# A hybrid decoder step: cached keys, convolution norm and opening put in another order

## The chip, the cores and the metric

The kernel runs on one core of one Trainium2 chip, as one program of some 14,900 instructions. The metric is the device time of one execution in microseconds; three executions of the kernel before gave 653.95, 655.58 and 656.63 us, median 655.58.

The core's engines each run their own list of instructions in order: PE (TensorE, matrix products), DVE (VectorE), ACT (ScalarE), POOL (GpSimd) and SP (SyncE, which here issues every DMA). They wait for each other by semaphores.

## The reference, cut to what matters

Two layers of a decoder for 512 prompt tokens and 8 samples of 4 tokens, all in float32. The change is in layer 0:

```python
q, k, v, g_att, u_a, u_b, g_conv = split(rms(x, norm_0) @ w_in_0)   # x: 544 x 1024
o_att  = attention of 8 heads: prompt tokens over themselves (causal),
         sample tokens over two cached pages of 128 keys and values each,
         found through page_table, and over their own 4 tokens
y      = conv1d(u_a * sigmoid(u_b), 31 taps, per channel) + conv_b
o_conv = silu(layernorm(y, conv_ln_g_0, conv_ln_b_0))
x      = x + concat(o_att * silu(g_att), o_conv * silu(g_conv)) @ w_out_0
```

Layer 1 is a gated linear recurrence (HGRN2) with a norm and two projections of its own; nothing of it is touched.

## The kernel before, in words

Tokens lie along the free axis: 544 columns in two halves of 272 (`HALF`, `HC`), with channels on the 128 partitions. A projection goes by weight tiles of 128 output columns. `wtile` (L127) loads one (tag `wr`, 3 buffers) and splits it in a high and a low part, the high one on ACT (L133), the low one on DVE (L134). `unit` (L137) makes one half of one output tile by 24 products (L142, L143, L144: high by high, high by low, low by high for 8 k-tiles) into a PSUM bank of tag `g`, of which there are 3. Attention scores use tag `s` (2 banks), transposes `t` (2), attention outputs `o` (1).

**Opening** (L247 to L311). `squares` (L256) sums the squares of x in four parts whose engine the tuples SQ and SQB give: `sqg` is a two-operand product on GpSimd (L186), `sqa` a Square on ACT (L180), `sqv` a product on DVE (L183). The parts are added at L265 (GpSimd), L266 and L267 (DVE). `norms` (L249) sums over partitions on PE (L252), takes the root on ACT and the reciprocal on DVE (L254): into `kr` for the first half, into `r1b` for the second. `rawsplit` (L270) makes the low part of the second half's x on DVE (L273), `wsplits` the low parts of the first two weight tiles (L282). `scaled` (L233, its product is L235) multiplies a finished PSUM tile by the norm: `ct` and `rs` are the results, and the PSUM bank is free only when they are made. `norm_a` (L285) multiplies the first half by its norm (L288).

**Middle of layer 0.** Four head pairs go through `prepkq`, `prepvg` and `attend` (L478: scores L484, mask L486, softmax, transposes of the probabilities L102, values L508), among them the convolution's inputs, `uconv`, and its taps on DVE. After the last `attend` (pair 3) stand `gates(0)` and `gates(1)`, two of four chunks of the convolution's gate (48 unit products each), then the layer norm of the convolution half by half: sum of channels, L565 on PE, subtraction and squares, L575 on PE, root, reciprocal. Then `gates(2)`, `gates(3)`, and a loop over chunks that makes the product with the gate (L582 to L595).

Then come the samples. The keys loop (L597) runs over two groups of four samples: 8 tiles of cached keys (tag `kn`, 8 buffers, 256 KB each; the page number is read by a TENSOR_LOAD on SP, L605, and the load is issued at L606), 32 products with the queries into a PSUM bank of tag `s` (L612), the mask (L616), the samples' own keys (L619), softmax and transposed probabilities `PT`. The values loop (L636) does the same with cached values: loads L646 into the same 8 `kn` buffers, products L639 and L651, then L661 gathers the heads. The layer norm's two accumulators take `kn` buffers too (L558), and so do the opening's squares and the two buffers of the convolution's state, which are in use till they are written out at L519 (`out_convs`). Then `w_out_0` is applied by units, and layer 1 follows.

**What sets the order.** The program is written once, in the order above; a scheduler with a model of the machine then sets each engine's list at build time, bound by `tc.issue_after` where the code names an instruction to come after. SP's list is in order too: a DMA that waits for its buffer holds all those behind it.

Of the kernel before, what the change touches and what calls it, by code (L numbers as in the profile page):

```python
# [13 lines left out]
AF = mybir.ActivationFunctionType  # L14
# [52 lines left out]
def hybrid_step(ctx, tc, xt_in, cache_kt, cache_v, conv_in, hgrn_in, page_table, par_in, k_norm_0,  # L67
# [59 lines left out]
    def wtile(w, col, k0=0, k1=KT):  # L127
        nk = k1 - k0
        raw = mk(wp, "wr", [128, nk, 128], 3)
        SP.dma_start(raw, w[col // 128, :, k0:k1, :])  # L130
        wh = mk(wp, "wh", [128, nk, 128], 3, F32R)
        wl = mk(wp, "wl", [128, nk, 128], 3, F32R)
        A.activation(wh, raw, AF.Copy)  # L133
        V.tensor_tensor(wl, raw, wh, op=ALU.subtract)  # L134
        return wh, wl, k0, k1

    def unit(w, a, hf):  # L137
        ps = bank("g", HALF)
# [18 lines left out]
    def vec(name, k=0):  # L157
        return vecs[:, vidx[name] + k:vidx[name] + k + 1]
# [15 lines left out]
    def mtile(key, dt=F32R):  # L174
        m_[key] = mk(hp, "m", [128, T], 2 * KT, dt)
        return m_[key]

    with tc.tile_pool(name="l0", bufs=1) as lp:
# [13 lines left out]
            V.tensor_scalar(xg[k][:, hs], xT[k][:, hs], vec("n0", k), None, op0=ALU.mult)  # L192

        SQ = (sqg, sqa, sqa, sqv)
        SQB = (sqg, sqa, sqa, sqv)
        XG = (xga, xgv, xga, xgv, xga, xgv, xga, xgv, )
        NM = (V, V, V, V, V, V, V, V, )
        xg = [mtile(("xg", k), F32) for k in range(KT)]
# [57 lines left out]
        def squares(hf):  # L256
            sq = []
            for i in range(4):
                q = mk(lp, "kn", [128, T], 8).rearrange("p (a t) -> p a t", a=2)
                (SQ, SQB)[hf][i](q, xTall[:, 2 * i:2 * i + 2, HC[hf]])  # L260
                sq.append(q)
                if hf == 0:
                    for k in (2 * i, 2 * i + 1):
                        XG[k](k, HC[0])
            G.tensor_tensor(sq[0], sq[0], sq[1], op=ALU.add)  # L265
            V.tensor_tensor(sq[2], sq[2], sq[3], op=ALU.add)  # L266
            V.tensor_tensor(sq[0], sq[0], sq[2], op=ALU.add)  # L267
            return sq[0]
# [266 lines left out]
        p3 = prepvg(*p3)  # L535
        taps(2)
        taps(3)
        pins = attend(*p3)
        gc = []

        def gates(c):
            w = wtile(w_in_0, 3072 + c * 128)
            g2 = up[c]
            for hf in range(2):
                with tc.issue_after(pins[0].ins):
                    ps = unit(w, h, hf)
                ps = scaled(ps, 1, 0) if hf else ps
                tg = mk(lp, "tb", [128, HALF], 3)
                A.activation(tg, ps, AF.Tanh, scale=0.5)
                V.scalar_tensor_tensor(g2[:, HC[hf]], tg, 1.0, ps, op0=ALU.add, op1=ALU.mult)  # L550
            gc.append(g2)

        gates(0)
        gates(1)
        rss = []
        at_ = [mk(lp, "kn", [128, T], 8) for _ in range(2)]
        accs = [[t[:, HC[hf]] for hf in range(2)] for t in at_]
        for hf in range(2):  # L558
            hs = HC[hf]
            acc = accs[0][hf]  # L560
            V.tensor_tensor(acc, cy[0][:, hs], cy[1][:, hs], op=ALU.add)
            for c in range(2, 4):
                V.tensor_tensor(acc, acc, cy[c][:, hs], op=ALU.add)
            pm = bank("g", HALF)
            PE.matmul(pm, ones, acc, start=True, stop=True)  # L565
            acc = accs[1][hf]
            for c in range(4):
                V.scalar_tensor_tensor(cy[c][:, hs], pm, -1.0 / 512, cy[c][:, hs], op0=ALU.mult, op1=ALU.add)
                sq = mk(lp, "ct", [128, HALF], 2) if c else acc
                A.activation(sq, cy[c][:, hs], AF.Square)  # L570
                if c:
                    V.tensor_tensor(acc, acc, sq, op=ALU.add)
            pq = bank("g", HALF)
            with tc.issue_after(pins[2 + hf].ins):
                PE.matmul(pq, ones, acc, start=True, stop=True)  # L575
            rs = mk(lp, "rs", [128, HALF], 2)
            A.activation(rs, pq, AF.Sqrt, scale=1.0 / 512, bias=eps)
            V.reciprocal(rs, rs)
            rss.append(rs)
        gates(2)  # L580
        gates(3)
        for c in range(4):  # L582
            tgs = []
            for hf in range(2):
                hs = HC[hf]
                V.scalar_tensor_tensor(cy[c][:, hs], cy[c][:, hs], vec("lg", c), rss[hf], op0=ALU.mult, op1=ALU.mult)
                V.tensor_scalar(cy[c][:, hs], cy[c][:, hs], vec("lb", c), None, op0=ALU.add)
                tg = mk(lp, "ct", [128, HALF], 2)
                A.activation(tg, cy[c][:, hs], AF.Tanh, scale=0.5)
                V.scalar_tensor_tensor(tg, tg, 1.0, cy[c][:, hs], op0=ALU.add, op1=ALU.mult)  # L590
                V.scalar_tensor_tensor(tg, tg, 0.25, gc[c][:, hs], op0=ALU.mult, op1=ALU.mult)
                tgs.append(tg)
            mh, ml = mtile(("h", 4 + c)), mtile(("l", 4 + c))
            for hf in range(2):
                split(mh[:, HC[hf]], ml[:, HC[hf]], tgs[hf])  # L595

        PTs = []  # L597
        for g in range(2):
            s = bank("s", 288)
            for j in range(2):  # L600
                kns = []
# [30 lines left out]
            A.activation(PT[:, :256], pT[:, :256], AF.Copy)  # L632
            A.activation(PT[:32, 256:384], pT[:32, 256:384], AF.Copy)
            PTs.append(PT)
        oms = []
        for g in range(2):  # L636
            PT = PTs[g]
# [443 lines left out]
```

## Time and profile before

| | us |
|---|---|
| three executions | 653.95, 655.58, 656.63 (median 655.58) |
| the profiled execution, its own time | 655.62 |
| its span, first to last instruction | 652.9 (2.7 lie around it) |
| PE busy | 629.5 (96%) |
| DVE busy | 524.8 (80%) |
| ACT busy | 365.5 (56%) |
| POOL busy | 62.7 (10%) |
| DMA, mean over the span | 108 GB/s |

The span is the execution on the time axis of the trace. Busy time of PE counts a product at the clock at which it ran; the trace shows that clock as a share of full speed (PEclk), where 1.00 is 2.4 GHz and 0.50 is 1.2 GHz.

### The profile page before, as it was taken

The numbers are of one execution on the slowest core, as the hardware profiler recorded it, in microseconds if no ns is written. First come the engines' busy times: TensorE is split into PE (matmuls) and PEld (weight loads), VectorE is DVE, ScalarE is ACT, GpSimd is POOL, SyncE is SP. The second block draws the span as 40 slices with busy tenths as digits, with TensorE's granted clock in tenths as the row PEclk, the third lists the DMA queues.
The fourth block names the chain that finished last, engine by engine and source line by source line (L and its number), as shares of the span: only waits on it lengthen the run. The fifth ranks groups of instructions, "written<-read, shape, count | busy, mean of one in ns | idle before, by whom it ended". The sixth has DMA issues, their size and how long they took to land.

```text
span 652.9 us, 14858 instructions
## 1 busy us (share of the span) xinstructions
PE 629.5 (96%) x5806; PEld 581.9 (89%) x5806; DVE 524.8 (80%) x1252; ACT 365.5 (56%) x908; POOL 62.7 (10%) x91
## 2 busy tenths in 40 slices
PE   8799999999999986999989999999999999999997
PEld 6699998997996855879989999999999999999997
DVE  6999989889889857666978988878787878866656
ACT  7344486487378674445755664646464646447321
POOL 6100000000100000000011211111111110121000
PEclk9799999999999997999999999999999999999999
DMA  8434311221242047446442232323223232322114
GB/s 297 121 82 111 113 56 66 84 83 65 80 84 81 22 139 241 155 143 213 162 146 102 70 113 84 107 93 102 99 99 102 84 117 69 115 78 94 46 58 149
DMA packets 39015, 70.56 MB, mean 108 GB/s; under 512 B 11938, under 2 KB 20642, under 8 KB 38946
## 3 DMA queue, kind: packets, MB, share of 16 engines
q1 hardware_dynamic: 38946, 69.63, 33.6%
q8 instruction: 45, 0.74, 0.5%
q14 instruction: 24, 0.20, 0.1%
HBM read 59.88 MB, written 9.73 MB: 107 GB/s over the span
## 4 chain that ended last, share of the span: by engine, by line
PE 88%; DVE 4%; DMA 3%; ACT 3%; SPq 1%; issue 1%; DVEq 0%; ACTq 0%
PE g L142 23%; PE g L143 23%; PE g L144 22%; PE t L102 5%; PE s L484 2%; PE o L508 2%; DMA kn<-in_cache_kt_dram 2%; PE o L952 1%; PE t L939 1%; PE s L847 1%; DMA kn<-in_cache_v_dram 1%; PE s L612 1%; PE s L853 1%; DMA xTall<-in_xt_dram 1%; PE o L954 1%
## 5 line engine op out<-in xcount | busy, mean ns | idle before, releaser
L142 PE MATMUL g<-h,wh 128*128 128x272 f32 x944 | 278.9, 296 | 5.3 <-DVE ct L235 2.7
L143 PE MATMUL g<-h,wh 128*128 128x272 f32 x944 | 277.9, 295 | 1.9 <-DVE h L273 1.7
L144 PE MATMUL g<-h,wl 128*128 128x272 f32 x944 | 275.4, 292 | 0.0
L142 PEld LDWEIGHTS g<-h,wh 128*128 128x128 f32 x944 | 179.7, 190 | 9.7 <-ACT f L743 3.1
L143 PEld LDWEIGHTS g<-h,wh 128*128 128x128 f32 x944 | 179.6, 190 | 6.0 <-DVE h L273 3.1
L144 PEld LDWEIGHTS g<-h,wl 128*128 128x128 f32 x944 | 179.5, 190 | 1.7 <-issue 1.2
L133 ACT ACTIVATE wh<-wr 128x1024 fp32r<-128x1024 f32 (+4 forms) x90 | 88.1, 981 | 91.1 <-PE g L143 84.5
L134 DVE TENSOR_TENSOR wl<-wr,wh 128x1024 fp32r<-128x1024 f32 (+4 forms) x90 | 101.1, 1125 | 26.4 <-ACT wh L133 25.6
L379 DVE SCALAR_TENSOR_TENSOR m<-m,vecs,m 128x512 f32<-128x512 f32 x120 | 87.5, 741 | 0.7
L142 PE MATMUL g<-m,wh 128*128 128x272 f32 x256 | 74.0, 293 | 0.3 <-ACT wh L133 0.3
L144 PE MATMUL g<-m,wl 128*128 128x272 f32 x256 | 74.1, 291 | 0.0
L143 PE MATMUL g<-m,wh 128*128 128x272 f32 x240 | 69.6, 290 | 0.0
L142 PEld LDWEIGHTS g<-m,wh 128*128 128x128 f32 x256 | 47.9, 188 | 2.6 <-DVE m L106 0.8
L144 PEld LDWEIGHTS g<-m,wl 128*128 128x128 f32 x256 | 48.1, 189 | 1.0 <-issue 0.8
L143 PEld LDWEIGHTS g<-m,wh 128*128 128x128 f32 x240 | 45.2, 188 | 1.1 <-DVE ct L590 0.8
L959 ACT ACTIVATE S<-S,tot 128x128 f32<-128x128 f32 x64 | 20.5, 390 | 11.4 <-PE t L858 11.4
L484 PE MATMUL s<-kz,qT 128*128 128x128 f32 (+3 forms) x64 | 22.8, 447 | 1.4 <-ACT PP L496 1.3
L916 DVE TENSOR_TENSOR qq<-qq,tot 128x256 f32<-128x256 f32 x24 | 11.7, 486 | 14.8 <-PE s L888 12.0
L503 ACT ACTIVATE PT<-t 128x128 f32<-128x128 f32 (+3 forms) x32 | 13.9, 433 | 14.7 <-PE t L102 14.6
L961 POOL TENSOR_TENSOR ve<-vx,cst 128x1024 fp32r<-128x1024 f32 x8 | 16.1, 2019 | 49.8 <-DVE vx L736 30.0
L1020 DVE TENSOR_TENSOR xTall<-g,xTall 128x272 f32<-128x272 f32 x32 | 13.5, 437 | 8.8 <-PE g L144 8.3
L917 DVE TENSOR_TENSOR kk<-kk,tot 128x256 f32<-128x256 f32 (+1 forms) x48 | 20.0, 417 | 0.3
(300 smaller groups left out, 1018.6 us busy)
## 6 DMA issues: line engine op xcount, KB each, us to landing
wr<-in_w_in_dram SPq DMA_DIRECT2D x58, 512.0 KB, 3.6
wr<-in_w_out_dram SPq DMA_DIRECT2D x16, 512.0 KB, 3.7
kn<-in_cache_kt_dram SPq DMA_DIRECT2D x16, 256.0 KB, 3.6
kn<-in_cache_v_dram SPq DMA_DIRECT2D x16, 256.0 KB, 4.7
S<-in_hgrn_dram SPq DMA_DIRECT2D x8, 512.0 KB, 4.8
out_hgrns_dram<-S SPq DMA_DIRECT2D x8, 512.0 KB, 2.6
xTall<-in_xt_dram SPq DMA_DIRECT2D x8, 272.0 KB, 5.4
out_y_dram<-xTall SPq DMA_DIRECT2D x8, 272.0 KB, 2.1
```

The costliest lines, as they stand in the source:

```text
L102: PE.transpose(out, in_, ident[:np_, :np_])
L133: A.activation(wh, raw, AF.Copy)
L134: V.tensor_tensor(wl, raw, wh, op=ALU.subtract)
L142: PE.matmul(ps, wh[:, k - k0, :], ah, start=(k == k0), stop=False)
L143: PE.matmul(ps, wh[:, k - k0, :], al, start=False, stop=False)
L144: PE.matmul(ps, wl[:, k - k0, :], ah, start=False, stop=(k == k1 - 1))
L379: V.scalar_tensor_tensor(cy[c][:, :TP], up[c][:, j:j + TP], cw[:, c, j:j + 1], cy[c][:, :TP], op0=ALU.mult, op1=ALU.add)
L484: sc = PE.matmul(ss[hh][:, :L], qT[:, i * 128:(i + 1) * 128], kT[:, hh, 0:L], start=True, stop=False)
L503: A.activation(PT[:, :L], pT[:, :L], AF.Copy)
L917: V.tensor_tensor(k3[:, :, 0, :], k3[:, :, 0, :], t3[:, :, 1:2].to_broadcast([128, nblk, hsz]), op=ALU.mult)
L959: A.activation(S0[:, n], S0[:, n], AF.Copy, scale=tots[:, n:n + 1])
L961: G.tensor_tensor(ve, vx.unsqueeze(1).to_broadcast([128, NS, 128]), exm.unsqueeze(2).to_broadcast([128, NS, 128]), op=ALU.mult)
```

## The change: keys(0) first, the norm in two parts, no GpSimd additions

Opening: the first quarter of the second half's squares goes from GpSimd to ACT (SQB); the addition L265 goes from GpSimd to DVE, for both halves; three casts of constants (L313, L315, L317) go from GpSimd to ACT.

Keys: the body of the keys loop becomes `keys(g)`. `keys(0)` is called ahead of the last pair's `attend`, `keys(1)` where the loop stood.

Norm: the means and squares of both halves come first, then `gates(2)`, then root and reciprocal of both halves, then `gates(3)`. The accumulators take tag `kr` (2 buffers) in place of `kn`.

```diff
-        SQB = (sqg, sqa, sqa, sqv)
+        SQB = (sqa, sqa, sqa, sqv)
...
-            G.tensor_tensor(sq[0], sq[0], sq[1], op=ALU.add)
+            V.tensor_tensor(sq[0], sq[0], sq[1], op=ALU.add)
...
-        G.tensor_copy(identb, ident)
+        A.activation(identb, ident, AF.Copy)
...
-        G.tensor_copy(causb, cst[:, C_CAUS:C_CAUS + 128])
+        A.activation(causb, cst[:, C_CAUS:C_CAUS + 128], AF.Copy)
...
-        G.tensor_copy(smb, cst[:, C_SM:C_SM + 64])
+        A.activation(smb, cst[:, C_SM:C_SM + 64], AF.Copy)
...
+        def keys(g):
...
+        keys(0)
         pins = attend(*p3)
         gc = []
...
-        at_ = [mk(lp, "kn", [128, T], 8) for _ in range(2)]
-        accs = [[t[:, HC[hf]] for hf in range(2)] for t in at_]
+        accs = [mk(lp, "kr", [128, T], 2) for _ in range(2)]
...
                 if c:
                     V.tensor_tensor(acc, acc, sq, op=ALU.add)
+        gates(2)
+        for hf in range(2):
             pq = bank("g", HALF)
             with tc.issue_after(pins[2 + hf].ins):
-                PE.matmul(pq, ones, acc, start=True, stop=True)
+                PE.matmul(pq, ones, accs[1][:, HC[hf]], start=True, stop=True)
...
-        gates(2)
         gates(3)
...
-        for g in range(2):
+        keys(1)
```

In the changed file the keys' loads are L548, their products L554, mask and own keys L558 and L561, the norm's products L605 and L617, the values' loads L650.

How the scheduler's order changes is shown at three places. Numbers after an underscore tell tiles of one name apart.

First, DVE in the opening, where the norm of the first half (`kr_107`) is applied to the first two PSUM tiles (`g_156`, `g_170`). Before:

```order
L273 SCALAR_TENSOR_TENSOR h_93<-xTall,vecs,h_85 128x272
L267 TENSOR_TENSOR kn_195<-kn_195,kn_199 128x544
L273 SCALAR_TENSOR_TENSOR h_94<-xTall,vecs,h_86 128x272
L254 RECIPROCAL kr_107<-kr_107 128x272
L273 SCALAR_TENSOR_TENSOR h_95<-xTall,vecs,h_87 128x272
L134 TENSOR_TENSOR wl_357<-wr_354,wh_356 128x1024
L254 RECIPROCAL r1b<-r1b 128x272
L235 TENSOR_TENSOR ct_214<-g_156,kr_107 128x272
L235 TENSOR_TENSOR rs_216<-g_170,kr_107 128x272
```

With the change:

```order
L254 RECIPROCAL kr_107<-kr_107 128x272
L267 TENSOR_TENSOR kn_195<-kn_195,kn_199 128x544
L273 SCALAR_TENSOR_TENSOR h_93<-xTall,vecs,h_85 128x272
L273 SCALAR_TENSOR_TENSOR h_94<-xTall,vecs,h_86 128x272
L273 SCALAR_TENSOR_TENSOR h_95<-xTall,vecs,h_87 128x272
L134 TENSOR_TENSOR wl_357<-wr_354,wh_356 128x1024
L235 TENSOR_TENSOR ct_214<-g_156,kr_107 128x272
L235 TENSOR_TENSOR rs_216<-g_170,kr_107 128x272
L288 TENSOR_TENSOR tb_218<-m_99,kr_107 128x272
L288 TENSOR_TENSOR tb_222<-m_100,kr_107 128x272
L288 TENSOR_TENSOR tb_226<-m_101,kr_107 128x272
L254 RECIPROCAL r1b<-r1b 128x272
```

The reciprocal of the second half, `r1b`, stood ahead of the two L235 and stands now behind them and three L288. Each L265, not shown here, stands some rows further up on DVE, the second one behind the first two L273.

Second, PE in attention, where before the keys of both groups (`s_3091`, `s_3242`) follow the last values product (L508) of pair 3:

```order
L508 MATMUL o_2563<-PT_2684,vt_2421 64x128
L508 MATMUL o_2563<-PT_2698,vt_2421 64x128
L508 MATMUL o_2563<-PT_2684,vt_2421 64x128
L508 MATMUL o_2563<-PT_2698,vt_2421 64x128
L612 MATMUL s_3091<-kn_3125,qbd 32x128
L612 MATMUL s_3091<-kn_3114,qbd 32x128
L612 MATMUL s_3091<-kn_3103,qbd 32x128
L612 MATMUL s_3091<-kn_3092,qbd 32x128
```

With the change the end of keys(0), whose PSUM tile is `s_2563`, stands ahead of the first scores of pair 3 (`s_2715`):

```order
L554 MATMUL s_2563<-kn_2657,qbd 32x128
L554 MATMUL s_2563<-kn_2646,qbd 32x128
L102 MATMUL t_2296<-cst,PP_2292 128x128 x4
L554 MATMUL s_2563<-kn_2635,qbd 32x128
L554 MATMUL s_2563<-kn_2624,qbd 32x128
L558 LDWEIGHTS identb
L558 MATMUL s_2563<-smb,identb 128x32
L561 MATMUL s_2563<-ksT,qbd 32x32 x16
L484 MATMUL s_2715<-kz_486,qT_2092 128x128
L486 LDWEIGHTS identb
```

The 32 products of keys(0) run from 42 rows above these last ones, among the last transposes and L508 of pair 2. Those of keys(1) (`s_3242`) stand as 8 after both L605, 12 between the two L617 and 12 after the units of `gates(3)`, followed by the values.

Third, SP around the cached keys. Before, all 16 loads stand behind the fourth tile of `w_out_0`:

```order
L130 DMA wr_3614<-in_w_out_dram 128x1024
L130 DMA wr_3647<-in_w_out_dram 128x1024
L382 DMA out_convp_dram<-m_275 128x30
L464 DMA out_v_prompt_dram<-vt_2421 128x4x128
L465 DMA out_v_sample_dram<-vsn 32x128
L130 DMA wr_3682<-in_w_out_dram 128x1024
L130 DMA wr_3717<-in_w_out_dram 128x1024
L606 ISA
L606 DMA kn_3092<-in_cache_kt_dram 128x512
```

With the change:

```order
L519 DMA out_convs_dram<-kn_268 128x16x30
L548 ISA
L548 DMA kn_2657<-in_cache_kt_dram 128x512
L130 DMA wr_3032<-in_w_in_dram 128x1024
L130 DMA wr_3106<-in_w_in_dram 128x1024
L439 DMA out_k_prompt_dram<-kt_2069 128x4x128
L440 DMA out_k_sample_dram<-kt_2069 32x128
L130 DMA wr_3614<-in_w_out_dram 128x1024
L130 DMA wr_3647<-in_w_out_dram 128x1024
L548 ISA
L548 DMA kn_3243<-in_cache_kt_dram 128x512
```

Six loads of keys(0) are not in this piece: they stand in the opening, behind `wr_492`, and the seventh behind the first `out_convs`. The eighth (`kn_2657`) stands right behind the second `out_convs`, which writes out the buffer that it takes. The eight of keys(1) stand behind two tiles of `w_out_0`, no longer four.

## Rows read from the trace of the kernel before

**Rows 1.** The page, part 1: busy us, share of the span, instructions.

```profile
PE 629.5 (96%) x5806; PEld 581.9 (89%) x5806; DVE 524.8 (80%) x1252; ACT 365.5 (56%) x908; POOL 62.7 (10%) x91
```

**Rows 2.** Timeline of PE, opening: start us, us, engine, line, tiles [idle<-releaser].

```profile
25.98 0.59 PE L142 MATMUL g<-h,wh 128*128 128x272 f32 x1 [2.68 <-DVE ct L235]
```

**Rows 3.** Windows of four stretches: us, PE, PEld, DVE, ACT, POOL, PEclk, DMA, GB/s.

```profile
21.00:23.30 2.30, 1.43 (x8) 0.92 (x6) 2.30 (x3) 0.57 (x2) 0.11 (x1) 1.00 0.07 29
23.30:25.90 2.60, 0.01 (x1) 0.00 (x0) 2.60 (x4) 0.98 (x1) 0.00 (x0) 0.77 0.00 0
25.90:31.30 5.40, 5.32 (x23) 5.32 (x24) 5.02 (x13) 1.57 (x4) 0.00 (x0) 0.50 0.34 114
60.00:100.00 40.00, 40.00 (x319) 38.87 (x318) 36.99 (x73) 24.62 (x47) 0.22 (x1) 1.00 0.32 100
```

**Rows 4.** Timeline of DVE in the opening.

```profile
7.52 1.27 DVE L192 TENSOR_SCALAR m<-xTall,vecs 128x272 f32<-128x272 f32 x1 [0.89 <-DMA xTall<-in_xt_dram]
...
9.35 0.35 DVE L192 TENSOR_SCALAR m<-xTall,vecs 128x272 f32<-128x272 f32 x1
...
11.08 3.25 DVE L282 TENSOR_TENSOR wl<-wr,wh 128x1024 fp32r<-128x1024 f32 x2
14.25 2.47 DVE L273 SCALAR_TENSOR_TENSOR h<-xTall,vecs,h 128x272 fp32r<-128x272 f32 x3
...
17.32 0.49 DVE L273 SCALAR_TENSOR_TENSOR h<-xTall,vecs,h 128x272 fp32r<-128x272 f32 x1
17.73 0.71 DVE L266 TENSOR_TENSOR kn<-kn,kn 128x544 f32<-128x544 f32 x1
...
22.66 1.21 DVE L134 TENSOR_TENSOR wl<-wr,wh 128x1024 fp32r<-128x1024 f32 x1
23.80 1.84 DVE L254 RECIPROCAL r1b<-r1b 128x272 f32<-128x272 f32 x1
```

**Rows 5.** Timeline of POOL (GpSimd) in the opening.

```profile
7.07 1.34 POOL L265 TENSOR_TENSOR kn<-kn,kn 128x544 f32<-128x544 f32 x1 [1.47 <-ACT kn L180]
...
11.07 2.17 POOL L186 TENSOR_TENSOR kn<-xTall 128x544 f32<-128x544 f32 x1 [2.43 <-DMA xTall<-in_xt_dram]
13.32 2.21 POOL L265 TENSOR_TENSOR kn<-kn,kn 128x544 f32<-128x544 f32 x1
```

**Rows 6.** Timeline of PE, end of the third head pair.

```profile
212.82 0.49 PE L484 MATMUL s<-kz,qT 128*128 128x128 f32 x2 [0.62 <-ACT PP L496]
```

**Rows 7.** Timeline of PE around the keys and the convolution norm.

```profile
241.47 0.66 PE L102 MATMUL t<-cst,PP 128*128 128x128 f32 x4 [1.13 <-ACT PP L498]
242.26 0.73 PE L575 MATMUL g<-kn,ones 128*128 128x272 f32 x2
...
245.55 1.08 PE L612 MATMUL s<-kn,qbd 128*32 128x128 f32 x32 [1.08 <-DMA kn<-in_cache_kt_dram]
249.62 1.62 PE L612 MATMUL s<-kn,qbd 128*32 128x128 f32 x32 [2.99 <-DMA kn<-in_cache_kt_dram]
...
253.88 1.94 PE L612 MATMUL s<-kn,qbd 128*32 128x128 f32 x32 [1.91 <-DMA kn<-in_cache_kt_dram]
255.75 1.24 PE L575 MATMUL g<-kn,ones 128*128 128x272 f32 x2
```

**Rows 8.** Timeline of PE around the cached values.

```profile
270.38 0.46 PE L619 MATMUL s<-ksT,qbd 128*32 128x32 f32 x32
...
272.46 1.12 PE L639 MATMUL s<-vsn,PT 32*128 32x512 f32 x2
...
277.95 1.06 PE L651 MATMUL s<-kn,PT 128*32 128x512 f32 x8 [0.58 <-DMA kn<-in_cache_v_dram]
```

**Rows 9.** Timeline of SP, which issues the DMAs.

```profile
179.56 0.38 SPq L519 DMA_DIRECT2D out_convs_dram<-kn  x1
...
239.00 17.16 SPq L606 DMA_DIRECT2D kn<-in_cache_kt_dram  x16
...
270.34 2.00 SPq L646 DMA_DIRECT2D kn<-in_cache_v_dram  x4
```

More of the change, by code (lines that the diff above doesn't have):

```diff
@@ L537, in hybrid_step @@
         taps(3)
[L538 to L551, printed above, removed]
@@ L553, in hybrid_step @@
-        gates(0)
-        gates(1)
-        rss = []
-        at_ = [mk(lp, "kn", [128, T], 8) for _ in range(2)]
-        accs = [[t[:, HC[hf]] for hf in range(2)] for t in at_]
[L558 to L574, printed above, removed]
-                PE.matmul(pq, ones, acc, start=True, stop=True)
[L576 to L579, printed above, removed]
@@ L580, in hybrid_step @@
-        gates(2)
[L581 to L595, printed above, removed]
@@ L634, in hybrid_step, with gates @@
             PTs.append(PT)
+        keys(0)
+        pins = attend(*p3)
+        gc = []
+        def gates(c):
+            w = wtile(w_in_0, 3072 + c * 128)
+            g2 = up[c]
+            for hf in range(2):
+                with tc.issue_after(pins[0].ins):
+                    ps = unit(w, h, hf)
+                ps = scaled(ps, 1, 0) if hf else ps
+                tg = mk(lp, "tb", [128, HALF], 3)
+                A.activation(tg, ps, AF.Tanh, scale=0.5)
+                V.scalar_tensor_tensor(g2[:, HC[hf]], tg, 1.0, ps, op0=ALU.add, op1=ALU.mult)
+            gc.append(g2)
@@ new lines, in hybrid_step @@
+        gates(0)
+        gates(1)
+        rss = []
+        accs = [mk(lp, "kr", [128, T], 2) for _ in range(2)]
+        for hf in range(2):
+            hs = HC[hf]
+            acc = accs[0][:, hs]
+            V.tensor_tensor(acc, cy[0][:, hs], cy[1][:, hs], op=ALU.add)
+            for c in range(2, 4):
+                V.tensor_tensor(acc, acc, cy[c][:, hs], op=ALU.add)
+            pm = bank("g", HALF)
+            PE.matmul(pm, ones, acc, start=True, stop=True)
+            acc = accs[1][:, hs]
+            for c in range(4):
+                V.scalar_tensor_tensor(cy[c][:, hs], pm, -1.0 / 512, cy[c][:, hs], op0=ALU.mult, op1=ALU.add)
+                sq = mk(lp, "ct", [128, HALF], 2) if c else acc
+                A.activation(sq, cy[c][:, hs], AF.Square)
+                if c:
+                    V.tensor_tensor(acc, acc, sq, op=ALU.add)
@@ new lines, in hybrid_step @@
+        gates(2)
+        for hf in range(2):
+            pq = bank("g", HALF)
+            with tc.issue_after(pins[2 + hf].ins):
+                PE.matmul(pq, ones, accs[1][:, HC[hf]], start=True, stop=True)
+            rs = mk(lp, "rs", [128, HALF], 2)
+            A.activation(rs, pq, AF.Sqrt, scale=1.0 / 512, bias=eps)
+            V.reciprocal(rs, rs)
+            rss.append(rs)
+        gates(3)
+        for c in range(4):
+            tgs = []
+            for hf in range(2):
+                hs = HC[hf]
+                V.scalar_tensor_tensor(cy[c][:, hs], cy[c][:, hs], vec("lg", c), rss[hf], op0=ALU.mult, op1=ALU.mult)
+                V.tensor_scalar(cy[c][:, hs], cy[c][:, hs], vec("lb", c), None, op0=ALU.add)
+                tg = mk(lp, "ct", [128, HALF], 2)
+                A.activation(tg, cy[c][:, hs], AF.Tanh, scale=0.5)
+                V.scalar_tensor_tensor(tg, tg, 1.0, cy[c][:, hs], op0=ALU.add, op1=ALU.mult)
+                V.scalar_tensor_tensor(tg, tg, 0.25, gc[c][:, hs], op0=ALU.mult, op1=ALU.mult)
+                tgs.append(tg)
+            mh, ml = mtile(("h", 4 + c)), mtile(("l", 4 + c))
+            for hf in range(2):
+                split(mh[:, HC[hf]], ml[:, HC[hf]], tgs[hf])
```

## The prediction, made before the changed kernel ran

> **What bounds the kernel now.** I read the page's busy shares first: PE is busy 96% of the span, some 23 us short of all of it [rows 1]. A change that takes no product away can therefore win little more than PE's idle time and the time in which PE ran at half clock. So the next view is PE's own timeline, read for the idle time in front of each instruction and for what ended it. The two largest clusters lie where the change works. In the opening PE stops for 2.68 us until DVE has made `ct` at L235 [rows 2]. Around 241 to 256 it stops four times, 1.13, 1.08, 2.99 and 1.91 us, once for the softmax of the last pair and three times for cached keys that have not landed [rows 7]. The windows view tells the second part of the price: PEclk is 1.00 up to 23.3, 0.77 on the mean of the 2.68 us stop, and 0.50 for 5.40 us after it, the lower of the two levels [rows 3]. The same shows in the keys: 32 products that take 1.08 us at the first wait take 1.62 and 1.94 after the 2.99 us one [rows 7]. So each long stop is paid twice. Between 60 and 100 PE has no gap at all [rows 3], and nothing is to be had there.
>
> **The opening.** L235 reads a PSUM tile and frees its bank; the product at 25.98 needs that bank. DVE works without a pause ahead of it, so L235 comes as much earlier as DVE's list ahead of it gets shorter.
> - GpSimd's three two-operand pieces (7.07, 11.07 and 13.32) go [rows 5]. The DVE work that ran beside them is long: L192 1.27 us where one alone takes 0.35, two L282 3.25 where the same shape at L134 takes 1.21 each, three L273 2.47 where one alone takes 0.49 [rows 4, 5]. If they run at the lone price, 0.9, 0.8 and 1.0 us go: −2.7. The nearest other reading is that they were slow for a reason of their own, then this is 0.
> - The reciprocal `r1b`, 1.84 us, stood ahead of L235 and now stands behind it [rows 4]: −1.8. Nothing needs it before the next L235, which belongs to the product after.
> - DVE gets two additions L265. Their price is that of L266, the same shape: 0.71 [rows 4]. The second costs it in full. The first falls into the 0.89 us that DVE waits for x in front of 7.52 [rows 4]; GpSimd could start it at 7.07 [rows 5], so some 0.2 remains. Together +0.9.
> - ACT gets one square and three casts. It is busy 0.57 and 0.98 us of the 2.30 and 2.60 ahead of the stop [rows 3], so they cost nothing; without that cover they would delay a weight split by about a microsecond.
>
> That makes −3.6: the product starts at about 22.4. PE gets two new, shorter stops on the way, since the second half's norm now waits on DVE's L267: by my walk down DVE's list about 1.7 us and 0.6 us. The decision is whether they drop the clock. The 2.68 us stop did [rows 2, 3]; between 21.0 and 23.3 PE was busy only 1.43 of 2.30 us, and the clock stayed at 1.00 [rows 3]. I take the row that is nearer in total idleness, the second: no drop. Then the products between 25.9 and 31.3 run at the full rate: 24 of them in 5.40 us are 0.225 each, 319 in 40.00 are 0.125 [rows 3], so another −2.4. Against it stands DVE, 5.02 busy of those 5.40 us and 36.99 of 40 later [rows 3]: a PE that is 6 us ahead must be followed by DVE, whose reserve is some 3 us in 40. I take 1.3 us as given back (bounds 0 and 3). **Opening: −3.6 − 2.4 + 1.3 = −4.7**, between −1 and −6.4.
>
> **The keys and the norm.** Of the 16 key tiles, loaded from 239.0 in 17.16 us behind four tiles of `w_out_0` [rows 9], seven now land far ahead; the eighth is a rival below. The six loads in the opening add 1.5 MB to a stretch in which the DMA engines moved 29 and 0 GB/s [rows 3], and their page numbers are read by SP as before. The loads of keys(1) wait only for keys(0)'s buffers, which come free some 20 us before their products. So three DMA waits go, and the softmax wait at 241.47 is filled with the units of `gates(2)`, which now stand ahead of that transpose: 1.13 + 1.08 + 2.99 + 1.91 = −7.1 [rows 7]. With the 2.99 us stop its half clock goes: 0.54 + 0.86 on the keys, and 1.24 against 0.73 on the two L575: −1.9 [rows 7].
>
> keys(0) itself is only moved. It stands where PE waits 0.62 us for probabilities [rows 6], and fills that; but its softmax holds one of two score banks, which the second score of pair 3 needs, for about as long. I take 0, between −0.6 and +1.5. The norm in two parts moves root and reciprocal behind 48 unit products (6 us of cover) and makes DVE do nothing more.
>
> What is late next is the cached values. They need the buffers of keys(1), so they are issued when its last product is done. Before, issue began at 270.34 and the product that needed them came at 277.95 after a wait [rows 8, 9]: 7.6 us. In the new order PE has less to do in that time: the own keys 0.46, L639 1.12, the first L651 1.06 [rows 8] and 26 unit products of 0.125, 5.9 together, so 1.7 us of wait. The second group's later half is issued when that L651 is done; until its own L651 stand 19 unit products (2.4), L661 (about an L639, 1.1), three transposes (0.5, by the four of [rows 7]), L639 and half the L651 (1.1 each), 6.2 together: 1.4 us of wait. Before, this stretch had 0.58 [rows 8]. So +2.5, between 0 and +5 (other loads beside them). Of these the price 7.6 is the measured one. By the Trainium skill (DMA: Bandwidth & Descriptors, Specifications) SP's path takes about 0.6 us to the first byte, and HBM gives one core about 358 GB/s; four tiles, 1.05 MB, would by that be an estimated 3.5 us, and both waits would be nothing. The rows say twice that, and I follow them.
>
> **Middle: −7.1 − 1.9 + 2.5 = −6.5**, between −3 and −10.
>
> Layer 1 stands in the same order as before and only comes earlier. The sum is −11.2 against the profiled execution's 655.6, which stands at the median of the three runs (655.58): **644.4 us**.
>
> **The rivals.**
> - *Loads as fast as the memory allows.* If the values land in the time of their bytes, the 3.1 us of waits in the sum go: 641.3. Against it stand the 7.6 us of the rows [rows 8, 9].
> - *The opening gives nothing.* Its two new stops, 2.3 us in a stretch of some 5, drop the clock as the 2.68 us did, and DVE, which is nearly full there, eats the start that came earlier. Only the middle remains: 655.6 − 6.5 = 649.1. For it speaks PEclk 0.77 within one stop [rows 3]. By the Trainium skill (TensorE: Matmul & The Clock Gate, Part 1) "the default state is throttled, and activity releases the throttle", so a thin stretch would do it without one long stop; the 1.43 us in 2.30 at 1.00 [rows 3] do not show that.
> - *The middle gives nothing.* The waits for keys come back as waits for values, softmax banks or weight tiles behind the earlier loads in SP's queue: 655.6 − 4.7 = 650.9. For it: all 16 value tiles still go through the same eight buffers. Against it: weight tiles are loaded ahead, and 48 products of 0.125 per tile are 6 us each.
> - *Nothing to measure.* The scheduler has moved half of PE's list; if small waits spread over it eat what both parts win, the time stays within 3.3 us of 655.6. Against it: PE was gapless in such stretches before [rows 3].
> - *Slower.* The eighth tile `kn_2657` takes the buffer that the second `out_convs` writes out. That write was issued at 179.56 [rows 9]; write and load, at 7.6 us each, end at about 195. PE needs it at about 206, where pair 2 ends, and all behind it on PE waits with it. From 206 on each microsecond later is lost, and by 220 the 11.2 us are used up and 3.3 more lost: 659 and over. Nothing moves `out_convs` by 25 us in DVE's order, so this is unlikely.
>
> **How the numbers follow.** About 0.5% (3.3 us) is what a measurement of this kernel can tell from no change. Chances: the forecast 0.50, fast loads 0.08, opening lost 0.16, middle lost 0.10, nothing to measure 0.11, slower 0.05. So faster 0.84, same 0.11, slower 0.05. The range reaches from the fast loads with the better opening, 639.0, to the middle lost, 651.0; it leaves out the last two cases. The forecast's own range is 641 to 648.
>
> **What the new profile would show.** Right: no stop of 2.7 us for L235, the first unit products after it at about 22.4 with PEclk 1.00; DVE's L282 at 1.2 and L273 at 0.5; no wait of the keys' products for a DMA; 240 to 256 without a gap; one or two waits of 1 to 2 us in front of L651. Wrong: PEclk 0.50 somewhere before 30; a wait for the eighth tile near 206; more than 5 us of waits for values; DVE as the releaser of many small PE waits between 30 and 200.

## The result, and the profile after

The changed kernel takes 643.64 us (median of four executions, 641.23 to 647.24) against 654.81 of the kernel before in the same runs: ratio 0.9842, 95% interval 0.9818 to 0.9865. The two medians lie 11.2 us apart, and the ratio makes it 10.3 us (8.8 to 11.9); forecast were 11.2. The profiled execution took 643.47, its span is 641.6 against 652.9.

Where it came from is read from one fixed place. The two norm products that close layer 0, one per half, are L685 before and L689 now; the last record of the second starts at 339.2 before and at 328.1 now. So 11.1 of the 11.3 us that the span lost lie ahead of it, and layer 1 gave 0.2. The first scores of pair 0, which close the opening, start at 83.20 before and at 77.70 now: 5.5 us are from the opening and the other 5.6 from the middle.

The page's first part, beside [rows 1]: PE is busy for 3.5 us less, though its instructions are the same 5806, since fewer of them ran at half clock.

```profile
PE 626.0 (98%) x5806; PEld 580.0 (90%) x5806; DVE 522.2 (81%) x1254; ACT 367.5 (57%) x912; POOL 52.1 (8%) x85
```

**The opening.** PE's timeline of the changed kernel, beside [rows 2]:

```profile
19.55 1.16 PE L252 MATMUL t<-kn,ones 128*128 128x272 f32 x4 [1.97 <-DVE kn L267]
...
22.52 0.40 PE L142 MATMUL g<-h,wh 128*128 128x272 f32 x1 [0.80 <-DVE ct L235]
```

The product behind L235 starts at 22.52, 3.5 us earlier. The new stop in front of L252 is there too, 1.97 us, and another of 0.80. The windows, as in [rows 3] (us, PE, PEld, DVE, ACT, POOL, PEclk, DMA share, GB/s), show that they cost no clock, although PE was busy for only 0.58 of 2 us in the first and 1.20 of 2 in the third:

```profile
17.00:19.00 2.00, 0.58 (x5) 0.36 (x3) 2.00 (x2) 1.29 (x3) 0.59 (x1) 1.00 1.12 156
...
21.00:23.00 2.00, 1.20 (x9) 0.98 (x8) 2.00 (x4) 1.29 (x2) 0.00 (x0) 1.00 0.83 259
23.00:25.00 2.00, 2.00 (x19) 2.00 (x17) 2.00 (x4) 1.13 (x3) 0.00 (x0) 1.00 0.79 247
```

DVE's timeline, beside [rows 4], shows the prices without GpSimd beside it:

```profile
7.34 0.73 DVE L265 TENSOR_TENSOR kn<-kn,kn 128x544 f32<-128x544 f32 x1 [0.39 <-ACT kn L180]
7.99 0.36 DVE L192 TENSOR_SCALAR m<-xTall,vecs 128x272 f32<-128x272 f32 x1
...
10.56 2.35 DVE L282 TENSOR_TENSOR wl<-wr,wh 128x1024 fp32r<-128x1024 f32 x2
12.83 0.91 DVE L273 SCALAR_TENSOR_TENSOR h<-xTall,vecs,h 128x272 fp32r<-128x272 f32 x2
13.66 0.72 DVE L265 TENSOR_TENSOR kn<-kn,kn 128x544 f32<-128x544 f32 x1
...
22.03 0.43 DVE L235 TENSOR_TENSOR ct<-g,kr 128x272 f32<-128x272 f32 x1
```

L192 takes 0.36 us where it took 1.27, two L282 2.35 where they took 3.25, and each L265 about 0.72, as forecast from L266.

**The middle.** PE's timeline, beside [rows 6] and [rows 7] (in the changed file the keys' products are L554, the norm's L605 and L617, the values' L643 and L655):

```profile
204.49 1.50 PE L554 MATMUL s<-kn,qbd 128*32 128x128 f32 x44 [0.21 <-ACT PP L496]
```

```profile
233.23 1.08 PE L605 MATMUL g<-kr,ones 128*128 128x272 f32 x4
...
244.51 0.86 PE L554 MATMUL s<-kn,qbd 128*32 128x128 f32 x24
...
253.19 0.86 PE L554 MATMUL s<-kn,qbd 128*32 128x128 f32 x24
```

```profile
268.29 1.06 PE L655 MATMUL s<-kn,PT 128*32 128x512 f32 x8 [0.67 <-DMA kn<-in_cache_v_dram]
...
274.56 1.00 PE L142 MATMUL g<-m,wh 128*128 128x272 f32 x3 [1.31 <-ACT m L105]
```

No product of the keys waits for a DMA any more. The windows of the same stretch show no idle time from 240 to 260, and then what came in exchange: 1.4 us of idle time between 270 and 275, and the clock at 0.50 for some 6 us.

```profile
240.00:250.00 10.00, 10.00 (x98) 8.59 (x97) 5.67 (x9) 7.94 (x12) 0.00 (x0) 1.00 0.44 149
250.00:260.00 10.00, 10.00 (x120) 7.83 (x118) 9.53 (x20) 4.56 (x7) 0.00 (x0) 1.00 0.59 193
260.00:265.00 5.00, 4.67 (x36) 3.49 (x36) 4.75 (x14) 2.47 (x8) 0.00 (x0) 1.00 0.94 322
...
270.00:275.00 5.00, 3.58 (x25) 3.06 (x24) 4.51 (x17) 2.73 (x10) 0.00 (x0) 0.96 0.01 3
275.00:280.00 5.00, 4.86 (x20) 4.22 (x20) 4.27 (x7) 3.91 (x6) 0.00 (x0) 0.50 0.12 41
```

SP's timeline, beside [rows 9]: the eighth tile was issued at 181.10, when the write in front of it had landed, and the eight tiles of keys(1) at 205.58, 28 us ahead of their first product. The values behind them go from 245.17 on, the last twelve tiles at 254.06 and 261.13.

```profile
181.10 0.35 SPq L548 DMA_DIRECT2D kn<-in_cache_kt_dram  x1
...
205.58 5.16 SPq L548 DMA_DIRECT2D kn<-in_cache_kt_dram  x8
...
254.06 4.95 SPq L650 DMA_DIRECT2D kn<-in_cache_v_dram  x8
...
261.13 2.34 SPq L650 DMA_DIRECT2D kn<-in_cache_v_dram  x4
```

### The profile page after: what moved, and what is told of

Its sections match the earlier page's. It is cut to its first block, busy times and chain, and to the rows that moved or that the text cites. A ratio compares the mean times of both kernels' runs of the same rounds, so it can differ in the third digit from the quotient of the medians.

```text
span 641.6 us, 14859 instructions
## 1 busy us (share of the span) xinstructions
PE 626.0 (98%) x5806; PEld 580.0 (90%) x5806; DVE 522.2 (81%) x1254; ACT 367.5 (57%) x912; POOL 52.1 (8%) x85
## 4 chain that ended last, share of the span: by engine, by line
PE 87%; DVE 5%; ACT 3%; DMA 2%; issue 1%; SPq 1%; DVEq 0%; ACTq 0%
PE g L142 23%; PE g L143 22%; PE g L144 22%; PE t L102 5%; PE s L484 2%; PE o L508 2%; DMA wr<-in_w_in_dram 1%; PE o L956 1%; PE t L943 1%; PE s L851 1%; PE s L857 1%; PE o L958 1%; PE s L554 1%; DMA kn<-in_cache_v_dram 1%; PE t L862 1%
## 5 line engine op out<-in xcount | busy, mean ns | idle before, releaser
L142 PE MATMUL g<-m,wh 128*128 128x272 f32 x256 | 74.7, 299 | 1.4 <-ACT m L105 1.3
L143 PE MATMUL g<-m,wh 128*128 128x272 f32 x240 | 70.7, 296 | 0.1
L142 PEld LDWEIGHTS g<-m,wh 128*128 128x128 f32 x256 | 48.7, 193 | 4.4 <-issue 1.7
L143 PEld LDWEIGHTS g<-m,wh 128*128 128x128 f32 x240 | 46.4, 194 | 0.7 <-DVE m L106 0.3
```

## The experiments

Each kernel computes everything. "Close" is the place named above, the last record of the norm product that closes layer 0, in the profiled execution; what lies behind it took 312.0 to 315.2 us in these traces. Ratios are to the kernel before, run beside each on the same chip; its medians there were 654.07 to 656.18, so ratios and closes compare better than the medians of different rows.

| kernel | median us | ratio (95%) | close, us |
|---|---|---|---|
| before | 654.81 | 1 | 339.2 |
| the change | 643.64 | 0.9842 (0.9818 to 0.9865) | 328.1 |
| opening alone | 649.67 | 0.9917 (0.9891 to 0.9943) | 334.1 |
| middle alone | 650.43 | 0.9920 (0.9896 to 0.9945) | 332.6 |
| change, norm in its old order | 650.31 | 0.9909 (0.9880 to 0.9939) | 333.8 |
| change, keys(0) late | 643.26 | 0.9794 (0.9767 to 0.9822) | 327.4 |
| opening and kr accumulators alone | 649.61 | 0.9930 (0.9911 to 0.9949) | 332.6 |
| opening and split norm alone | 642.98 | 0.9827 (0.9806 to 0.9848) | 326.6 |
| change, accumulators in kn | 642.94 | 0.9817 (0.9797 to 0.9836) | 327.9 |
| opening alone, norm products in t | 647.24 | 0.9896 (0.9871 to 0.9921) | 331.7 |
| change, GpSimd's work back | 650.27 | 0.9928 (0.9905 to 0.9952) | 334.8 |
| change, L659 held back | 639.47 | 0.9778 (0.9761 to 0.9794) | 323.7 |
| the same, lb on ACT | 638.39 | 0.9767 (0.9744 to 0.9789) | 322.1 |
| the same, keys(0) late | 638.98 | 0.9756 (0.9736 to 0.9776) | 323.3 |

### The two halves apart

Opening alone: the first five edits of the change, on the kernel before.

> The opening's edits alone, the middle as before. Theory A, two separate gains: in the trace with the change the product behind L235 starts 3.5 us earlier and the 24 products behind it run at the full clock (2.4 us), and the third head pair's rows are then 5.5 to 6.7 us early, so DVE gives nothing back. By A this kernel takes 654.8 - 5.9 = 649 us, the product starts at 22.5 with a wait under 1 us, and PEclk is 1.00 till 35. Rival B, DVE gives back what PE gains, and the early rows come only from a reordered list: 651.5 to 653 us, with new waits of PE for DVE between 30 and 200.

Middle alone: the changed kernel with those five edits undone.

```diff
-        SQB = (sqa, sqa, sqa, sqv)
+        SQB = (sqg, sqa, sqa, sqv)
...
-            V.tensor_tensor(sq[0], sq[0], sq[1], op=ALU.add)
+            G.tensor_tensor(sq[0], sq[0], sq[1], op=ALU.add)
...
-        A.activation(identb, ident, AF.Copy)
+        G.tensor_copy(identb, ident)
```

> Keys and norm as in the change, the opening as before. Theory A: 654.8 - 5.3 = 649.5 us; the three waits for cached keys are gone, and the half clock after 274 of the changed kernel (a wait of 1.3 us for the last chunk of the convolution, then 6 us at 0.50) is there, some 6 us later. Rival B, the middle needs the opening (with the six key loads in a free stretch of SP and DVE's list early): under 3 us of gain, 652 us or more, with key tiles late. Rival C, the half clock at 274 is a by-product of the early opening and is not here: 646 to 647 us.

The closes are 5.1 and 6.6 us early, 11.7 together, and the change's is 11.1 early: the two halves add (A). Of the 6.6, 0.9 stand already at pair 0 (82.33 for 83.20), from the scheduler's other order; so 5.7 are the middle's own, as the change's 5.6. In the opening alone pair 0's first scores stand at 77.66, as in the change, so DVE gave nothing back there. The 0.4 us between 5.5 and 5.1 are less than the waits for keys grew with an earlier PE: 1.25, 3.46 and 2.65 us, 7.4 in all, where the kernel before had 1.08 + 2.99 + 1.91 [rows 7].

In the middle alone the stop for the convolution's last chunk is there, 1.32 us, as in the change; but the clock holds (that part of C is seen, its total is not):

```profile
280.85 0.65 PE L142 MATMUL g<-m,wh 128*128 128x272 f32 x3 [1.32 <-ACT m L105]
```

```profile
280.00:282.00 2.00, 1.15 (x8) 1.10 (x9) 1.53 (x5) 0.99 (x3) 0.00 (x0) 1.00 0.00 0
282.00:284.00 2.00, 1.05 (x6) 0.61 (x6) 2.00 (x4) 2.00 (x3) 0.00 (x0) 1.00 0.00 0
```

### Which edit of the middle it is

Norm in its old order, keys(0) early:

```diff
-        gates(2)
-        for hf in range(2):
             pq = bank("g", HALF)
...
             rss.append(rs)
+        gates(2)
         gates(3)
```

> The changed kernel with the convolution's norm in its old order: half by half with root and reciprocal, then the gate chunks 2 and 3; keys(0) stays early, and the accumulators stay in their new buffers. Theory A: the early keys carry the gain of the middle (6.0 us of waits for keys and 1.4 of half clock) and the split norm only fills one wait of 1.1 us: 643.6 + 1 to 2, 644.6 to 645.6 us. Rival: the norm in two parts is what keeps PE filled between 240 and 255; without it PE waits twice for root and reciprocal (two table loads of 1.3 us and 1.85 us each on the way): 647 us or more, with PEclk falling there.

Keys(0) late, norm split:

```diff
-        keys(0)
         pins = attend(*p3)
...
+        keys(0)
         keys(1)
```

> The changed kernel with keys(0) called right ahead of keys(1), where the loop stood; the split norm and the new opening stay. Theory A: the key tiles are late again, or, since all 8 buffers are free of accumulators, four to eight of them are early and the second eight late: 3 to 6 us lost, 647 to 650 us, with a wait of PE for cached keys of 2 us or more. Rival: with the accumulators out of the keys' buffers the first eight tiles land early wherever the call stands, and the last eight hide behind the gate chunks: within 1 us of 643.6.

Theory A, by which the early keys carry the middle, does not hold. With early keys and the old norm the close is 5.7 us later than in the change, though no product waits for keys. PE runs out of other work instead: 99 unit products stand in a row behind the last norm product, from 253.11 on (98 from 253.64 in the opening alone). Ahead of them PE waits 1.12 us for values and 0.73 for DVE, and the clock falls; behind them the convolution's chunks come late, PE waits for them three times, and the clock falls again (0.51 from 280 to 285).

```profile
250.00:255.00 5.00, 5.00 (x20) 3.07 (x21) 2.10 (x6) 1.24 (x2) 0.00 (x0) 0.50 0.46 172
```

```profile
275.20 0.64 PE L142 MATMUL g<-m,wh 128*128 128x272 f32 x3 [0.59 <-ACT m L105]
...
277.85 0.65 PE L142 MATMUL g<-m,wh 128*128 128x272 f32 x3 [1.14 <-ACT m L105]
...
280.49 1.05 PE L142 MATMUL g<-m,wh 128*128 128x272 f32 x3 [1.14 <-ACT m L105]
```

With keys(0) late and the split norm nothing is lost. But only half of the loads are late here: the first eight go as early as in the change, as the rival expected, and the second eight from 243.72 and 250.91. PE waits 1.50 us for these, without a drop of the clock:

```profile
18.86 6.50 SPq L548 DMA_DIRECT2D kn<-in_cache_kt_dram  x6
...
243.72 2.03 SPq L548 DMA_DIRECT2D kn<-in_cache_kt_dram  x4
...
250.91 2.37 SPq L548 DMA_DIRECT2D kn<-in_cache_kt_dram  x4
```

```profile
257.27 1.08 PE L554 MATMUL s<-kn,qbd 128*32 128x128 f32 x32 [1.50 <-DMA kn<-in_cache_kt_dram]
```

Later PE waits 1.18 and 0.92 us for values, and the clock is 0.84 on the mean from 270 to 275; the stop for the convolution's last chunk is gone. These waits stand in the place of the change's.

So the question became whether the new buffers or the split norm carry it. Buffers alone, on the opening alone:

```diff
-        at_ = [mk(lp, "kn", [128, T], 8) for _ in range(2)]
+        at_ = [mk(lp, "kr", [128, T], 2) for _ in range(2)]
```

> The new opening, and of the middle one thing alone: the norm's two accumulators take the two kr buffers; norm and keys stand as before the change. With all eight keys' buffers free, SP issues the first eight key loads early, though the keys loop is where it was. Theory D, the norm's place between the gate chunks is what fills PE: key waits of the first group go, but root and reciprocal of the norm, the last chunks and the values wait without cover, 648 to 651 us (the opening alone gave 649.7, the changed kernel without the split norm 650.3). Rival, the buffers carry it: 644 to 646 us, and the split of the norm only repairs what the early keys(0) spoils.

Split norm alone: keys(0) late as above, and the accumulators back in the keys' buffers.

```diff
-        accs = [mk(lp, "kr", [128, T], 2) for _ in range(2)]
+        accs = [mk(lp, "kn", [128, T], 8) for _ in range(2)]
```

> The new opening, and of the middle the split norm alone: the accumulators are back in two of the keys' eight buffers, and keys(0) stands where the loop stood. Theory D: the split norm is what wins, because gate chunk 2 gets its PSUM banks ahead of the second pair of norm products, so that 48 unit products fill the norm's latency; late keys are harmless as long as PE has units: 643 to 645 us. Theory E, buffers and split are both needed: in this order all 16 key loads stand behind the third tile of w_out_0 and behind the accumulators' release, which come only with the second norm products; then PE waits for key tiles 4 us or more behind the units and the clock falls: 648 to 650 us. The early keys alone were worth nothing (643.3 without them).

The last diff alone, on the change (keys(0) early):

> The changed kernel with only the accumulators back in the keys' buffers: keys(0) early, norm split. Theory D: two of the eight tiles of keys(1) wait for the accumulators, which come free at the second norm product near 245, and their load then needs some 4 to 8 us; their products stand last, near 253 in the changed kernel: a wait of 0 to 3 us, 643.6 to 646.6 us. Theory E: the value loads behind them in SP's list come later too, and the tail loses 4 us or more: 648 us.

D, by which the norm's place carries the middle, holds in all three; the last two come out 0.02 and 0.7 us under its ranges. The buffers alone bring the first eight loads forward, since SP finds their buffers free whether keys(0) is called early or not; PE still stops for the second eight, and runs their products at half clock. The close is 1.5 us earlier than in the opening alone, the median the same.

```profile
244.57 1.93 PE L612 MATMUL s<-kn,qbd 128*32 128x128 f32 x32 [3.19 <-DMA kn<-in_cache_kt_dram]
```

The split norm alone gives 642.98, the whole result. It does so with all 16 loads late; PE has work until 257.9, then waits 1.76 us, the only wait for keys, and the clock stays full:

```profile
250.00:255.00 5.00, 5.00 (x119) 4.43 (x118) 5.00 (x15) 2.45 (x4) 0.00 (x0) 1.00 0.25 71
```

```profile
259.63 1.08 PE L554 MATMUL s<-kn,qbd 128*32 128x128 f32 x32 [1.76 <-DMA kn<-in_cache_kt_dram]
```

E, both needed, falls with it, and with the split norm the keys' place and buffers are worth nothing that these runs can tell.

### Why the split norm works

In the old order the units of gate chunks 2 and 3 take PSUM tiles of tag g behind the norm's four products, and there are three such banks. The test gives the norm another tag and leaves the order as it was:

```diff
-            pm = bank("g", HALF)
+            pm = bank("t", HALF)
...
-            pq = bank("g", HALF)
+            pq = bank("t", HALF)
```

> The new opening with the old middle (late keys, norm half by half ahead of gate chunks 2 and 3, accumulators in the keys' buffers), and one edit: the norm's four products go to PSUM tiles of tag t, no longer of tag g. In the old middle the units of chunks 2 and 3 take the g banks behind those four, so they stand behind the last norm product; here they do not, and PE's list has them ahead of and between the norm products. Theory F, the g banks' turn is why the split norm wins: the units fill the time before 256, and the kernel comes to 643 to 646 us, some 4 to 6 less than the opening alone (649.7). Rival G, the banks are not the reason, PE's units are then merely used up earlier and the norm's latency and the keys wait open behind them: 648 to 651 us, with waits for keys or for the convolution's chunks near 260 and PEclk at 0.50 there.

647.24 lies between the two theories: 2.4 us less than the opening alone, of 6.7 that the split norm gives (2.4 of 7.5 at the close). The units do move ahead of the norm, so their turn for a bank did hold them (F). But the scheduler then runs nearly all of them ahead of the second norm product, and the keys' loads and the norm's chain open behind them (G):

```profile
252.36 1.61 PE L612 MATMUL s<-kn,qbd 128*32 128x128 f32 x32 [2.69 <-DMA kn<-in_cache_kt_dram]
...
255.90 1.27 PE L575 MATMUL t<-kn,ones 128*128 128x272 f32 x2 [1.20 <-DVE kn L572]
258.77 1.93 PE L612 MATMUL s<-kn,qbd 128*32 128x128 f32 x30 [1.60 <-DMA kn<-in_cache_kt_dram]
```

```profile
255.00:260.00 5.00, 2.50 (x26) 1.64 (x29) 3.84 (x11) 4.32 (x8) 0.00 (x0) 0.50 0.96 345
```

Shown is that banks are a part of the cause. The rest may be the place of the units, one chunk ahead of the second norm products and one behind. But the split also shortens the norm's own chain, which this test left in its old order. In the opening alone the second half's subtraction stands on DVE behind the first half's reciprocal, which waits for the root on ACT, and the last square is added at 247.02:

```profile
238.59 1.85 DVE L578 RECIPROCAL rs<-rs 128x272 f32<-128x272 f32 x1 [2.38 <-ACT rs L577]
...
247.02 0.42 DVE L572 TENSOR_TENSOR kn<-kn,ct 128x272 f32<-128x272 f32 x1
```

With the split norm alone the last two are added from 239.57 on:

```profile
239.57 0.99 DVE L611 TENSOR_TENSOR kn<-kn,ct 128x272 f32<-128x272 f32 x2
```

ACT also loads a table (1.28 us each) twice there between 230 and 256, and four times in the opening alone. Both causes agree with these rows and with the 642.98; they were not tried apart.

### The opening's cause

The change with GpSimd's square and both additions back, the casts still on ACT:

```diff
-        SQB = (sqa, sqa, sqa, sqv)
+        SQB = (sqg, sqa, sqa, sqv)
...
-            V.tensor_tensor(sq[0], sq[0], sq[1], op=ALU.add)
+            G.tensor_tensor(sq[0], sq[0], sq[1], op=ALU.add)
```

> The changed kernel with GpSimd's two-operand work of the opening back: the square's quarter of the second half and both additions L265 on GpSimd, the casts still on ACT. In its order the reciprocal of the second half stands behind the two L235, as in the change. Collision theory: DVE's L192, L282 and L273 beside GpSimd are long again (1.2, 3.2 for two, 0.6 and more), 2.7 us, less the 1.4 us of the two additions: L235 comes some 1.3 to 1.8 us later than in the change, at 23.5 to 24, and the wait of PE there is 2 us; if the clock falls, 647 us, if not, 645 us. Rival, the place of the reciprocal carries the opening: L235 at 22 to 22.5 and 643.6 us, DVE's rows short.

DVE's L192 (1.74 us) and two L282 (4.40) are long again, three L273 (1.32) are not, and L235 comes at 23.37 where it came at 22.03. PE waits 0.97 us there, not 2, and the clock falls all the same:

```profile
7.02 1.74 DVE L192 TENSOR_SCALAR m<-xTall,vecs 128x272 f32<-128x272 f32 x1 [0.43 <-DMA xTall<-in_xt_dram]
...
11.04 4.40 DVE L282 TENSOR_TENSOR wl<-wr,wh 128x1024 fp32r<-128x1024 f32 x2
...
23.37 0.43 DVE L235 TENSOR_TENSOR ct<-g,kr 128x272 f32<-128x272 f32 x1
```

```profile
25.00:26.00 1.00, 1.00 (x6) 1.00 (x6) 1.00 (x2) 0.67 (x2) 0.00 (x0) 0.50 0.95 274
```

So the collision is real, at 1.3 us and, with the clock, more: pair 0's first scores stand at 79.48, 1.8 us behind the change. But 3.7 of the opening's 5.5 us are still there, with the reciprocal `r1b` behind L235 as in the change; the collision accounts for a third of it. That the reciprocal's place gives the rest is argued from its 1.84 us; no run moved it alone. The rest of this kernel's loss lies elsewhere: its list came out with a stop of 2.28 us in pair 2 and a drop of the clock behind it (0.66 on the mean from 190 to 200), long after the pieces of GpSimd that were put back, which end at 14.36. So its 650.27 is no price of the opening.

```profile
193.19 1.22 PE L484 MATMUL s<-kz,qT 128*128 128x256 f32 x2 [2.28 <-ACT PP L496]
```

### What was left on the table

DVE's timeline of the changed kernel at the stop at 274.56 shows what stood ahead of the convolution's last chunk (L631, L632 and the split L106):

```profile
269.50 0.69 DVE L659 TENSOR_TENSOR P<-s,cst 128x512 f32<-128x512 f32 x1 [1.16 <-PE s L655]
...
272.43 0.49 DVE L106 TENSOR_TENSOR m<-oTs,m 128x32 fp32r<-128x32 f32 x4
...
274.54 0.79 DVE L106 TENSOR_TENSOR m<-ct,m 128x272 fp32r<-128x272 f32 x2 [0.20 <-ACT m L105]
```

L659 waits 1.16 us for the second group's values, and the four splits for the sample tokens (`oTs`) follow, which only the second half of `w_out_0` reads. First L659 is held back behind the last chunk's split:

```diff
-            V.tensor_tensor(om.rearrange("p (h d) -> p h d", d=64), ov.rearrange("p (h d) -> p h d", d=64),
...
+            with (tc.issue_after(last.ins) if g else nullcontext()):
+                V.tensor_tensor(om.rearrange("p (h d) -> p h d", d=64), ov.rearrange("p (h d) -> p h d", d=64),
...
```

(`last` is the last split of the product loop.)

> The changed kernel with one instruction of DVE held back: the second sample group's L659 (it reads the values product and in the changed kernel stands ahead of the convolution's last two chunks) comes after the last chunk's split. In the changed kernel DVE waited 1.16 us for PE there, and four small splits of the samples followed ahead of the last chunk, though only the second half of w_out_0 needs them. Theory: the last chunk is ready 2 to 2.5 us earlier, the wait of 1.31 us at 274.56 goes and with it the half clock (some 30 products, 3 us): 639 to 640 us. Rival: PE then waits for the held L659 at L665, in its order ahead of the unit products, and loses the same there: within 1 us of 643.6.

639.47: the stop is 0.59 us, the clock holds, and the close is 4.4 us earlier than in the change (0.3 of it already at pair 0).

```profile
272.09 0.64 PE L142 MATMUL g<-m,wh 128*128 128x272 f32 x3 [0.59 <-ACT m L105]
```

```profile
275.00:280.00 5.00, 4.94 (x39) 4.93 (x40) 4.59 (x12) 2.56 (x10) 0.00 (x0) 1.00 0.59 193
```

Then the addition of `lb` goes to ACT as well:

```diff
-                V.tensor_scalar(cy[c][:, hs], cy[c][:, hs], vec("lb", c), None, op0=ALU.add)
+                A.activation(cy[c][:, hs], cy[c][:, hs], AF.Identity, bias=vec("lb", c))
```

> As the run before, and the convolution's addition of lb (eight L628, 0.35 us each, 0.27 apart in the row) is made by ACT in place of DVE. DVE is busy 9.5 of 10 us between 250 and 260 in the changed kernel, ACT 4.6. Theory: the product loop ends 2 us earlier still; if the wait at 274 is already gone nothing more is won, 639 us; if it is only shortened, 0.5 to 2 us more than the run before. Rival: ACT's list, in order, delays the weight splits there and the gain turns into waits for wh: slower than the run before.

638.39, close 1.6 us earlier again; its waits for values and for the convolution are gone from PE's list of waits. The medians of these two runs differ by less than their spread, and the trace is that of the fastest execution (635.96), so no gain is shown for this step. Last, the same with keys(0) late:

> The best kernel so far (L659 held back, lb on ACT, 638.4 us) with keys(0) called right ahead of keys(1). Theory D: as with the changed kernel itself, the place of the call changes nothing that counts, 638.4 within 1 us. Rival: the waits of the late keys (1.5 us) and of the values behind them (2.1 us), which the late product loop hid there, now stand on the path: 640 to 642 us, with PEclk falling near 270.

638.98, D again: by the medians the place of keys(0) changes nothing that counts here either. The close is 1.2 us later, but against the trace of that fastest execution.

## Why the prediction was right, and where it was not

- **The sum.** 644.4 forecast, 643.64 measured. Of the halves, −4.7 and −6.5 forecast; in the change 5.5 us are gained ahead of pair 0's first scores and 5.6 behind them, so the opening gave more than forecast and the middle less. Two bounds do not follow from their terms: −3.6 and −2.4 with nothing given back make −6.0, not −6.4, and 641.3 less the 1.7 from −4.7 to −6.4 is 639.6, not 639.0. Nothing hangs on either.
- **Opening, start of the product.** 22.4 forecast, 22.52 measured, and the clock kept full as chosen. Both new stops were met (1.7 and 0.6 forecast, 1.97 and 0.80 found). Of the 1.3 us given back by DVE at most 0.5 came: 5.5 of the 6.0 us are there at pair 0. Collisions less additions were priced at 2.7 − 0.9 = 1.8 us at L235; with GpSimd's work back L235 is 1.3 us later. The other 2.2 us of L235's 3.5 agree with the reciprocal's place, priced at 1.8, which was not tried alone.
- **Middle, the term that failed.** "So three DMA waits go" booked 6.0 us of waits and 1.9 us of half clock to key tiles that land early. The waits went, so the amount is right; the reason is wrong. PE waited for keys since it had nothing else in its list: the units of chunks 2 and 3 stood behind the last norm product. The prediction saw the split norm as "6 us of cover" for root and reciprocal, priced it at the 1.13 us wait, and gave the rest to the keys. With the keys early and the norm old the close is 5.7 us later than in the change; with all 16 loads late and the norm split it is 1.5 us earlier.
- **Middle, the values.** 2.5 us more of waits were forecast, from 7.6 us between issue and use. Found was 0.67 in all, against 0.58 before. The later four tiles of the first sample group, issued from 254.06, were used at 260.06 without a wait, so 6.0 us were enough; the later four of the second group, issued from 261.13, were used at 268.29 after one, 7.2 us on. So the 7.6 was an upper end, and the first of the two waits fell away. Of the 7.2 us, 2.0 pass until SP has issued the fourth tile, at 263.1, and a load landed 4.8 us (median of the four) after its issue, while the DMA engines moved 322 GB/s (260 to 265) for these tiles and for loads issued before them. The estimate of 3.5 us from the Trainium skill (DMA: Bandwidth & Descriptors, Specifications) is for four tiles that have the memory to themselves; it is not met by the 7.2, and no run here shows such tiles alone.
- **Middle, what was not seen.** In the place of those waits stands DVE: 1.31 us for the convolution's last chunk and the half clock after it, 4.4 us in all by the kernel that holds L659 back, where 0.59 us of the stop are left. The prediction named no cover for the product loop, which had run beside the late keys. This miss and the waits that did not come (2.4 us, and DVE's 0.8) nearly cancelled; that the sum came out better than its terms was luck.
- **The rivals.** The eighth tile was harmless: issued at 181.10, used from 204.49 on, with a 0.21 us wait for ACT and none for it.

## What to carry to other kernels

A wait names what came last, not what is missing. Where an engine waits for a load with a list behind it that could run, ask what holds that list; here it was the place of the norm between the units, in part by the turn for PSUM banks, and moving the loads bought nothing. When a stage shrinks, every chain beside it loses that time as cover; the next stop is found by walking the chain that used to end last but one. And work that only a later half needs (here the sample tokens) should not stand ahead of what the next product needs.

## What the runs showed of the hardware that was not expected

- The clock did not follow the length of a stop. A stop of 1.97 us and one of 0.80 us in the opening of the change left it at 1.00; in the kernel with GpSimd's work back, where no stop there is over 0.97 us, it fell to 0.50 from about 24.5 to 28. At the end of the middle 1.31 us cost some 6 us at half clock in the change, and 1.32 us, followed by 0.51 and 0.43, none in the middle alone. The four executions of the change ran at mean clocks of 0.989 to 0.997, so the profiled one (0.991) does not speak for all of them. What decides it these runs don't tell.
- DVE beside GpSimd: two L282 took 2.35 us alone, 3.25 in the kernel before, where GpSimd's L186 and L265 beside them took 2.17 and 2.21 [rows 5], and 4.40 with GpSimd's work back, where these took 1.28 and 1.79. The two share the loss, and not each time alike.

```profile
10.79 1.28 POOL L186 TENSOR_TENSOR kn<-xTall 128x544 f32<-128x544 f32 x1 [2.19 <-DMA xTall<-in_xt_dram]
...
12.57 1.79 POOL L265 TENSOR_TENSOR kn<-kn,kn 128x544 f32<-128x544 f32 x1 [0.49 <-ACT kn L180]
```
